# A hybrid transformer layer on one core: four weight sums moved from the retention stage into attention, one transfer for the last head's token sum, a split order and six additions on another engine

## The chip, the core and the metric

The kernel runs on one core of a Trainium2 chip. A core has engines with queues of their own that work side by side: PE (TensorE, matrix products; PEld is its weight load), DVE (VectorE), ACT (ScalarE), POOL (GpSimd) and SP (SyncE, which only issues transfers here). Each engine works through its queue in order, and an instruction whose inputs are not there holds up everything behind it. Transfers run on 16 DMA engines; those issued by SP go through one queue (q1), those issued by POOL through another (q0). The metric is the device time of one execution in microseconds (us), lower is better.

## The reference, cut to what matters

One layer over 1024 latent tokens of width 1024, with 256 context tokens:

```
h   = rms_norm(x) * (1 + sc1) + sh1                 # latent; the context likewise
p   = h @ w_in                                      # columns for two head groups
ret = silu(rg) * (group_norm(retention forwards) + group_norm(retention backwards))   # 4 heads
dif = sub_norm((softmax(q1 k1) - lam * softmax(q2 k2)) @ v)                           # 4 heads
x   = x + g1 * (concat(ret, dif) @ w_out)
h2  = rms_norm(x) * (1 + sc2) + sh2
x   = x + g2 * ((silu(a) * b) @ w_down)             # a, b: the halves of conv3(h2 @ w_up)
out = rms_norm(x) * final_g
```

All is float32. A product of the large projections is made in three passes over operands that are split into a high and a low part.

## The kernel before, in words

The work runs in stages that overlap at their edges: modulation and norms, the projections by `w_in`, retention (about 335 to 435 us of the profiled execution), differential attention (445 to 640 us), the output projection by `w_out` with the gated residual and the second norm (640 to 740 us), then the MLP.

**The output projection as seven products.** The product of tokens and `w_out` is cut into 2x2 blocks, and a Strassen-like scheme makes seven block products instead of eight. It needs sums of blocks of the weights and sums of blocks of the tokens. Both are formed in DRAM by transfers that add to what lies there (`accum_op=ALU.add`). The weights' sums are in `ws_d[0..3]` (each 128x4x512 float32): `w_terms` lists eight such additions, two halves (`k` of 0 and 2) for each of four sums; the first two sums add a block of `w_out`, and the other two are chained: `ws_d[1] += ws_d[0]`, then `ws_d[3] += ws_d[1]`. The tokens' sums are in `t1_d` to `t4_d`; `t1_d` holds minus the first half of the tokens of retention plus the second half.

**Retention.** `Pair` treats two 128-token chunks of one head; 16 pairs run as a pipeline in `outputs()` beside the query projection: `score`, `output` (PE), `squares` (ACT, and a power on POOL, L288), `gate` (four operations on DVE, L293, and two on POOL, L295 and L296), `turn` (transposed on PE, copied on ACT, stored by SP, L309). For the second half of the tokens `turn` issues one more transfer on POOL's queue, which adds the piece to `t1_d` (L311). The last step of `gate`, `last_y`, is what a weight sum is ordered behind: after the gates of pairs 1, 2, 10, 11, 12 and 13 `outputs` issues eight weight sums on POOL (L366). Each pair's keys (`rk`, L257) and values with their gates (`kvo`, L242) are loaded by SP, whose queue is in order: a load of `kvo` waits for a buffer that POOL's L296 frees, and what stands behind it in SP's queue waits along.

**Attention.** 32 units (4 heads x 8 query tiles). The first loads of a unit's queries and keys (`load(0)`, L1018 and L1021) are issued by POOL behind `last_y` of the last pair. Iteration `n` of the loop runs the 24 operations of several units by the table `TAU`; PE, DVE, ACT and SP keep exactly the order of the program there (`in_order`), while POOL's is left to the scheduler. POOL makes two small operations of each unit (L983, an input of DVE's L986, and L987, the power behind it, which ACT's L990 waits for), loads, `joined_tokens` (sums of attention's tokens, L1130 and L1132) and the first weights' low parts (L1107, L1124). `issue_after(units[n - 5].pool_ins)` puts a transfer behind L987 of unit `n - 5` in POOL's queue.

**The output projection.** `out_step` makes one block product into four PSUM tiles, `out_weights` and `sum_operand` load and split its weights and tokens: ACT makes the high part (L1106, L1336), DVE the low one (L1107, L1337). `after=(freed,)` puts the low parts of `w4` and of the sum `t4_d` behind a residual update (`freed`) in DVE's queue. Two additions complete the last head of `t4_d` (L1333, on POOL), and `gate` multiplies a finished tile by `g1` (L1345) and adds it to the rows (L1346): on DVE everywhere but in the step of `w4`, where the addition is on POOL. `norm2` scales the finished rows (L115, a power on POOL at L116, and L1231 on DVE), and `turned0` and the steps behind it transpose them on PE (L1238) for the MLP.

## Time and profile before

| | us |
|---|---|
| median of 3 runs | 1375.2 (1374.64 to 1376.37) |
| the profiled execution's own time | 1374.97 |
| its span, from the first to the last instruction | 1373.2 |
| PE busy | 1350.2 (98% of the span) |
| DVE busy | 1001.5 (73%) |
| ACT busy | 749.1 (55%) |
| POOL busy | 351.8 (26%) |

"Busy" counts a pipelined matrix product until its modelled end, so a PE that is busy all the time may still be without a pause between products or with short ones that don't show; a wait that the profile lists for PE is time in which it had nothing to do. The chain that ended last is on PE for 81% of the span. The granted clock of TensorE was 0.998 over the execution.

### The profile page before, as it was taken

To read this page: it belongs to the slowest core of one execution; us is meant where nothing else is said; L and a number is where in the kernel's file an instruction comes from. 1 tells how busy PE (TensorE), PEld (TensorE's weight loads), DVE (VectorE), ACT (ScalarE), POOL (GpSimd) and SP (SyncE) were. 2 spreads that over 40 slices of the span, in tenths; PEclk is the share of its full clock that TensorE was granted. 3 is DMA by queue.
4 is the path that set the end of the run, shared out by engine and by line. 5 is a ranking of instruction groups with operands and counts; after the bars stand their busy time and mean duration, and the time that the engine had idled before them with its cause. 6 is when DMAs were issued, how large, how long until landed. Compare 5 with 4: busy or idle time off the path is not lost.

```text
span 1373.2 us, 19870 instructions
## 1 busy us (share of the span) xinstructions
PE 1350.2 (98%) x6978; PEld 1134.5 (83%) x6978; DVE 1001.5 (73%) x1508; ACT 749.1 (55%) x1429; POOL 351.8 (26%) x440
## 2 busy tenths in 40 slices
PE   9999999999999999999999999999999999999997
PEld 6788888888888799988877888888888888888886
DVE  4746874425775898997889986777766777798857
ACT  4643312434665789987437654455554555455543
POOL 1210005403777435543131222212222210000001
PEclk9999999999999999999999999999999999999999
DMA  9567897655877877745853898988888875963523
GB/s 362 218 252 245 288 325 232 202 171 157 212 199 189 186 168 141 145 93 154 333 165 92 200 224 218 232 223 214 208 221 215 208 193 171 375 217 110 176 92 123
DMA packets 130636, 279.71 MB, mean 204 GB/s; under 512 B 13716, under 2 KB 35220, under 8 KB 129624
## 3 DMA queue, kind: packets, MB, share of 16 engines
q1 hardware_dynamic: 100440, 212.99, 45.6%
q0 software_dynamic: 29520, 64.00, 25.4%
q10 hardware_dynamic: 576, 1.44, 0.3%
q8 instruction: 55, 0.90, 0.3%
q14 instruction: 45, 0.37, 0.1%
HBM read 212.04 MB, written 69.75 MB: 205 GB/s over the span
## 4 chain that ended last, share of the span: by engine, by line
PE 81%; DVE 7%; ACT 4%; POOL 3%; issue 3%; DMA 2%; SPq 0%; POOLq 0%; DVEq 0%; ACTq 0%
PE chain L133 6%; PE chain L134 6%; PE chain L135 6%; PE c L134 5%; PE c L133 5%; PE c L135 5%; PE pv L972 4%; PE pA L940 4%; PE pn L135 3%; PE pn L134 3%; PE pn L133 3%; PE pl L133 3%; PE pl L135 3%; PE pl L134 3%; PE third L133 3%; PE third L135 3%
## 5 line engine op out<-in xcount | busy, mean ns | idle before, releaser
L1263 POOL DMA_DIRECT2D cmb<-w_up x80 | 73.6, 1142 | 175.1 <-DMA cmb<-w_up 141.7
L133 PE MATMUL pl<-hT,whi 128*128 128x512 f32 x256 | 105.4, 412 | 0.0
L133 PE MATMUL chain<-T,whi 128*128 128x512 f32 x264 | 103.1, 391 | 0.0
L134 PE MATMUL chain<-T,whi 128*128 128x512 f32 x264 | 102.8, 389 | 0.0
L135 PE MATMUL chain<-T,wlo 128*128 128x512 f32 x264 | 102.2, 389 | 0.0
L943 DVE TENSOR_REDUCE mt<-pA 128x1 f32<-128x1280 f32 x64 | 95.2, 1488 | 7.5 <-PE pA L940 6.3
L135 PE MATMUL pl<-hT,wlo 128*128 128x512 f32 x256 | 100.1, 391 | 0.0
L134 PE MATMUL pl<-hT,whi 128*128 128x512 f32 x256 | 99.9, 390 | 0.0
L947 ACT ACTIVATE p<-pA,mt 128x1280 f32<-128x1280 f32 x64 | 85.5, 1336 | 11.2 <-DVE mt L943 9.1
L940 PE MATMUL pA<-ks,qhl 128*128 128x512 f32 (+1 forms) x384 | 89.6, 368 | 1.3 <-DMA ks<-dk 0.8
L133 PE MATMUL c<-whi,ghl 128*128 128x512 f32 x232 | 90.2, 389 | 0.0
L134 PE MATMUL c<-wlo,ghl 128*128 128x512 f32 x232 | 90.2, 389 | 0.0
L135 PE MATMUL c<-whi,ghl 128*128 128x512 f32 x232 | 90.2, 389 | 0.0
L1187 ACT CAST whi<-cmb 128x512 fp32r<-128x512 f32 x60 | 37.4, 625 | 83.0 <-PE chain L134 65.1
L940 PEld LDWEIGHTS pA<-ks,qhl 128*128 128x128 f32 x384 | 67.9, 189 | 13.7 <-DVE mt L943 1.2
L972 PE MATMUL pv<-va,aT 128*128 128x128 f32 x640 | 77.4, 276 | 1.3 <-DVE yT L1001 1.0
L972 PEld LDWEIGHTS pv<-va,aT 128*128 128x128 f32 x640 | 74.0, 192 | 3.0 <-DVE yT L1001 2.1
L1187 ACT CAST whi<-wra 128x512 fp32r<-128x512 f32 x54 | 33.0, 622 | 71.7 <-PE third L134 42.3
L134 PE MATMUL third<-yT,whi 128*128 128x512 f32 x168 | 65.4, 389 | 0.0
L133 PE MATMUL third<-yT,whi 128*128 128x512 f32 x168 | 65.4, 389 | 0.0
L135 PE MATMUL third<-yT,wlo 128*128 128x512 f32 x168 | 65.4, 389 | 0.0
L133 PE MATMUL pn<-whi,hT 128*128 128x512 f32 x160 | 64.8, 405 | 0.0
(342 smaller groups left out, 3854.6 us busy)
## 6 DMA issues: line engine op xcount, KB each, us to landing
cmb<-w_up POOLq DMA_DIRECT2D x80, 256.0 KB, 6.5
wm<-w_mod SPq DMA_DIRECT2D x32, 512.0 KB, 5.7
cmb<-w_up SPq DMA_DIRECT2D x60, 256.0 KB, 5.4
raw<-w_in SPq DMA_DIRECT2D x27, 512.0 KB, 5.4
wra<-w_up SPq DMA_DIRECT2D x23, 512.0 KB, 6.2
W<-w_down SPq DMA_DIRECT2D x44, 256.0 KB, 5.5
wrb<-w_up SPq DMA_DIRECT2D x40, 256.0 KB, 3.8
ad<-s SPq DMA_DIRECT2D x20, 512.0 KB, 5.8
```

The lines of the kernel that those rows point to most:

```text
L133: mm(ps, lh, rh, start=first, stop=False, skip_group_check=more)
L134: mm(ps, lh, rl, start=False, stop=False, skip_group_check=more)
L135: return mm(ps, ll, rh, start=False, stop=last, skip_group_check=more)
L940: mm(self.pa[m][:, c0:c1], self.q[:, m, i, qs], self.k[:, m, c0:c1], start=(i == 0), stop=(i == 1))
L943: nc.vector.tensor_reduce(out=self.mt[:, m : m + 1], in_=self.pa[m][:, :LK], axis=AX.X, op=ALU.min)
L947: nc.scalar.activation(self.p[m], self.pa[m][:, :LK], AF.Exp, scale=-1.0, bias=self.mt[:, m : m + 1], accum_out=self.s[:, m : m + 1])
L972: mm(self.pv, self.aT[:, c, :], self.v[:, c, :], start=(c == 0), stop=(c == NKT - 1))
L1187: cast = nc.scalar.copy(hi, src)
L1263: nc.gpsimd.dma_start(out=o, in_=src, accum_op=ALU.add)
```

## The change

Five things are changed. (1) Two of the four weight sums, four of the eight transfers, leave the gates of pairs 10 to 13; they are issued in attention's iterations 15, 17, 21 and 28 instead. (2) The last head's two pieces of the second half are no longer added to `t1_d` one by one from `turn`; one transfer from DRAM to DRAM, `t1_d[:, 3] += yr_d[:, 3]`, does it in iteration 6, and the copy of `t1_d` to `t2_d` moves from iteration 8 to 9. (3) The first `joined_tokens` moves from iteration 11 to 12. (4) Of the four low parts of `w4`, and of the four of the sum `t4_d`, the first two are no longer put behind `freed`. (5) Six additions go from POOL to DVE: the two that complete the last head of `t4_d`, and the four residual additions in the step of `w4`.

```diff
-                if second:
+                if second and self.h < H - 1:
                     nc.gpsimd.dma_start(out=t1_d[:, self.h, o : o + 2 * P].rearrange("p (s l) -> p s l", s=2), in_=yr, accum_op=ALU.add)
...
-        w_terms = [(i, a, k) for i, a in ((0, A22), (2, A21), (1, ws_d[0]), (3, ws_d[1])) for k in (0, 2)]
+        w_terms = [(i, a, k) for i, a in ((0, A22), (2, A21)) for k in (0, 2)]
...
-                    for _ in range({1: 2, 2: 2, 10: 1, 11: 1, 12: 1, 13: 1}.get(n, 0)):
+                    for _ in range({1: 2, 2: 2}.get(n, 0)):
                         weight_sum(last_y[0])
...
-    def out_weights(srcs, sl, eng=nc.sync, low=nc.vector, lag=0, after=()):
+    def out_weights(srcs, sl, eng=nc.sync, low=nc.vector, lag=0, after=(), free=0):
...
-                for ins in after:
+                for ins in after if k - lag >= free else ():
                     order_only(part.ins, ins.ins)
...
-            if n == 8:
+            if n in (6, 9, 15, 17, 21, 28):
                 with tc.issue_after(units[n - 5].pool_ins.ins):
-                    nc.gpsimd.dma_start(out=t2_d[:, :, :], in_=t1_d[:, :, :])
+                    if n == 6:
+                        nc.gpsimd.dma_start(out=t1_d[:, H - 1, :], in_=yr_d[:, H - 1, :], accum_op=ALU.add)
+                    elif n == 9:
+                        nc.gpsimd.dma_start(out=t2_d[:, :, :], in_=t1_d[:, :, :])
+                    else:
+                        i, j, k = {15: (1, 0, 0), 17: (1, 0, 2), 21: (3, 1, 0), 28: (3, 1, 2)}[n]
+                        nc.gpsimd.dma_start(out=ws_d[i][:, k : k + 2, :], in_=ws_d[j][:, k : k + 2, :], accum_op=ALU.add)
...
-            for half, when in ((0, (11, 18, 26, 33)), (1, (16, 24, 31))):
+            for half, when in ((0, (12, 18, 26, 33)), (1, (16, 24, 31))):
...
-    def sum_operand(src, tt, half, turn=False, after=()):
+    def sum_operand(src, tt, half, turn=False, after=(), free=0):
...
-                nc.gpsimd.tensor_tensor(out=raw[:, 3, :], in0=raw[:, 3, :], in1=r32(yT[a][1][:, D // P - 1, :]), op=ALU.add)
+                nc.vector.tensor_tensor(out=raw[:, 3, :], in0=raw[:, 3, :], in1=r32(yT[a][1][:, D // P - 1, :]), op=ALU.add)
...
-            for ins in after:
+            for ins in after if k >= free else ():
                 order_only(part.ins, ins.ins)
...
-    w4 = weights(A22, freed)
-    sum_operand(t4_d, Y12, 1, after=(freed,))
+    w4 = weights(A22, freed, free=2)
+    sum_operand(t4_d, Y12, 1, after=(freed,), free=2)
...
-        gate(rows1[t], c1[t], right, ALU.subtract, nc.gpsimd)
+        gate(rows1[t], c1[t], right, ALU.subtract)
```

PE's queue holds the same instructions in the same order before and after. The scheduler places the others anew, and three places of the queues matter below.

The first is POOL's queue in the retention pairs 10 to 12 (`wsd` is `ws_d`, `qq`, `ss` and `y` are tiles of a pair). Before:

```order
L296 TENSOR_TENSOR y<-y,kvo 128x256
L366 DMA wsd_157<-wsd_156 128x1024
L288 TENSOR_TENSOR ss<-ss,mhalf 128x4
L295 TENSOR_TENSOR y<-o 128x256
L296 TENSOR_TENSOR y<-y,kvo 128x256
L366 DMA wsd_157<-wsd_156 128x1024
L266 TENSOR_TENSOR qq<-st,qd 128x512
```

and with the change:

```order
L296 TENSOR_TENSOR y<-y,kvo 128x256
L288 TENSOR_TENSOR ss<-ss,mhalf 128x4
L295 TENSOR_TENSOR y<-o 128x256
L296 TENSOR_TENSOR y<-y,kvo 128x256
L266 TENSOR_TENSOR qq<-st,qd 128x512
```

The transfers between the pairs' operations are gone; the operations themselves keep their order.

The second is POOL's queue at the end of retention, where attention's first queries (`qhl`) and keys (`ks`) are loaded; `sgd_152<-yr` is the addition to `t1_d`. Before:

```order
L296 TENSOR_TENSOR y<-y,kvo 128x256
L1018 DMA qhl<-dq_95 64x2x256
L311 DMA sgd_152<-yr 128x256
L1018 DMA qhl<-dq_95 64x2x256
L311 DMA sgd_152<-yr 128x256
L1021 DMA ks<-dk_99 64x1280 x2
L1018 DMA qhl<-dq_95 64x2x256 x2
L1021 DMA ks<-dk_99 64x1280 x2
```

and with the change:

```order
L296 TENSOR_TENSOR y<-y,kvo 128x256
L1018 DMA qhl<-dq_95 64x2x256 x2
L1021 DMA ks<-dk_99 64x1280 x2
L1018 DMA qhl<-dq_95 64x2x256 x2
L1021 DMA ks<-dk_99 64x1280 x2
```

The two additions no longer stand between the last gate and the keys.

The third is DVE's queue in the output projection, around the residual updates of the step of `w6` (the gates of `o_0` to `o_3`). Before:

```order
L1346 TENSOR_TENSOR x_2_6788<-x_2_6788,gated 128x512
L1346 TENSOR_TENSOR x_3_6789<-x_3_6789,gated 128x512
L1345 TENSOR_TENSOR gated<-o_0_6809,g_4494 128x512
L1345 TENSOR_TENSOR gated<-o_1_6810,g_4494 128x512
L1346 TENSOR_TENSOR x_0_6786<-x_0_6786,gated 128x512
L1346 TENSOR_TENSOR x_1_6787<-x_1_6787,gated 128x512
L1345 TENSOR_TENSOR gated<-o_2_6811,g_4494 128x512
L1345 TENSOR_TENSOR gated<-o_3_6812,g_4494 128x512
L1346 TENSOR_TENSOR x_2_6788<-x_2_6788,gated 128x512
L1346 TENSOR_TENSOR x_3_6789<-x_3_6789,gated 128x512
L1107 TENSOR_TENSOR wolo<-woraw,wohi 128x512 x4
L1337 SCALAR_TENSOR_TENSOR yT_4490<-raw_6794,yT_4488 128x512 x4
```

and with the change (lines 1339, 1343, 1351 and 1352 are the former 1333, 1337, 1345 and 1346):

```order
L1352 TENSOR_TENSOR x_3_6788<-x_3_6788,gated 128x512
L1107 TENSOR_TENSOR wolo<-woraw,wohi 128x512
L1339 TENSOR_TENSOR raw_6793<-raw_6793,yT_4482 128x512
L1343 SCALAR_TENSOR_TENSOR yT_4484<-raw_6793,yT_4482 128x512
L1339 TENSOR_TENSOR raw_6793<-raw_6793,yT_4484 128x512
L1107 TENSOR_TENSOR wolo<-woraw,wohi 128x512
L1343 SCALAR_TENSOR_TENSOR yT_4484<-raw_6793,yT_4482 128x512
L1351 TENSOR_TENSOR gated<-o_0_6808,g_4488 128x512
L1351 TENSOR_TENSOR gated<-o_1_6809,g_4488 128x512
L1352 TENSOR_TENSOR x_0_6785<-x_0_6785,gated 128x512
L1352 TENSOR_TENSOR x_1_6786<-x_1_6786,gated 128x512
L1351 TENSOR_TENSOR gated<-o_2_6810,g_4488 128x512
```

Two low parts of the weights and two of the tokens move ahead of these gates, with the two additions that were POOL's; the other two of each stay behind them.

More of the change, by code (lines that the diff above doesn't have):

```diff
@@ L1164 @@
                     units[v].run(o)
-                if op == "f" and n >= 9 and n not in (11, 16, 18, 24, 26, 31, 33):
+                if op == "f" and n >= 9 and n not in (12, 16, 18, 24, 26, 31, 33):
                     with tc.issue_after(units[min(n - 6, n_units - 1)].pool_ins.ins):
@@ L1319, in run, with weights @@
             pass
-    def weights(src, *after):
+    def weights(src, *after, free=0):
         sl = []
-        run(out_weights((src,), sl, after=after))
+        run(out_weights((src,), sl, after=after, free=free))
         return sl
-    def sum_operand(src, tt, half, turn=False, after=()):
+    def sum_operand(src, tt, half, turn=False, after=(), free=0):
         raw = raw0[:, 4 * half : 4 * half + 4, :]
```

## The prediction

> **What bounds the kernel now.** I read first the busy time of each engine by stretches of the execution, from the retention pairs to the MLP (the numbers in a row: its length, then the busy time and the instructions of PE, PEld, DVE, ACT, POOL, the granted clock, the DMA share, GB/s):
>
> ```profile
> 395.00:450.00 55.00, 52.19 (x285) 43.74 (x284) 30.02 (x58) 29.08 (x86) 38.88 (x44) 1.00 0.83 200
> 450.00:470.00 20.00, 18.23 (x105) 15.31 (x104) 18.48 (x22) 15.00 (x27) 9.81 (x10) 1.00 0.65 176
> 470.00:640.00 170.00, 168.89 (x1241) 155.80 (x1240) 153.00 (x203) 153.34 (x357) 78.13 (x123) 1.00 0.65 130
> 700.00:740.00 40.00, 35.07 (x173) 27.95 (x172) 32.53 (x60) 23.00 (x40) 14.22 (x15) 1.00 0.29 96
> 740.00:1360.00 620.00, 620.00 (x2742) 512.06 (x2741) 476.20 (x643) 323.71 (x488) 94.75 (x111) 1.00 0.73 200
> ```
>
> PE is the bound nearly everywhere, and its instructions do not change. So the change can only win what PE waits: 2.8 us in the first stretch, 1.8 in the second, 1.1 in attention, 4.9 in the fourth, none behind it. A saving on POOL or DVE counts where one of these waits ends on it. Second, PE's timeline names the waits (in brackets: the idle time before the row and what ended it):
>
> ```profile
> 408.44 0.68 PE L269 MATMUL pc<-xa,rk 128*128 128x128 f32 x4 [1.80 <-DMA rk<-rk]
> 449.16 1.40 PE L940 MATMUL pA<-ks,qhl 128*128 128x512 f32 x6 [0.83 <-DMA ks<-dk]
> 708.69 0.33 PE L1238 MATMUL pt<-ident,x 128*128 128x128 f32 x1 [0.21 <-DVE x L1231]
> 710.67 0.33 PE L1238 MATMUL pt<-ident,x 128*128 128x128 f32 x1 [1.66 <-DVE x L1231]
> 730.93 0.33 PE L1238 MATMUL pt<-ident,x 128*128 128x128 f32 x1 [0.83 <-DVE sm L115]
> 732.71 0.33 PE L1238 MATMUL pt<-ident,x 128*128 128x128 f32 x1 [1.45 <-DVE x L1231]
> 737.64 0.33 PE L1238 MATMUL pt<-ident,x 128*128 128x128 f32 x1 [0.79 <-DVE x L1231]
> ```
>
> Two are for transfers in retention; five, 0.21 + 1.66 + 0.83 + 1.45 + 0.79 = 4.94 us, are for the second norm, that is for DVE's queue. All seven lie where the change works.
>
> **Edit 1, the weight sums leave retention.** POOL's first sum, SP's load behind it, and the landing of the sums and of all `rk` loads:
>
> ```profile
> 398.89 0.86 POOL L366 DMA_DIRECT2D wsd<-wsd  x1
> 399.86 0.43 SPq L257 DMA_DIRECT2D rk<-rk  x1
> wsd<-wsd POOLq DMA_DIRECT2D x4, 512.0 KB, 8.4
> DMA to landing us min/median/max: 2.6/4.9/8.7
> ```
>
> The `rk` that PE waits for is issued at 399.86 and used at 408.44: about 8.5 us, where the median of ten such loads is 4.9. In that time the first 512 KB sum, which reads two operands and writes one, runs on the same DMA engines. Without it the load needs to come only 1.80 sooner, and the median is 3.6 sooner. So I take the whole **1.80 us**; the ends are 0 (the load is held by what SP issued ahead of it) and 1.80, since PE then has work. What is late next is the next pair's load, which goes out behind a POOL queue that is shorter by one sum.
>
> **Edit 2, one transfer for the last head.** POOL's queue at the end of retention:
>
> ```profile
> 435.21 0.95 POOL L311 DMA_DIRECT2D sgd<-yr  x1
> 437.23 0.88 POOL L311 DMA_DIRECT2D sgd<-yr  x1 [0.44 <-DMA yrd<-yr]
> 437.82 1.37 POOL L1021 DMA_DIRECT2D ks<-dk  x2
> ```
>
> The next rows start about 0.6 us behind each L311, and the second had a wait of 0.44 ahead of it: 0.6 + 0.44 + 0.6 = 1.6 us of the queue before the keys. PE's wait for the keys is 0.83. PE also arrives 1.80 earlier by edit 1; but POOL's four sums, about 0.6 us of its queue each, stood ahead of the same keys (2.4 us), and the keys also lose 256 KB of additions beside them. So the keys come some 4 us earlier against PE's 1.80: **0.83 us** goes, with ends of 0 (the keys move no more than PE does) and 0.83. PE's next waits, 1.77 us in the second stretch, are for DVE's and ACT's queues, which run from the same keys on, so they stay.
>
> **What edits 1 to 3 add to attention.** Five more issues on POOL (the copy to `t2_d` only moves), each behind a unit's L987:
>
> ```profile
> 534.92 2.40 PE L972 MATMUL pv<-va,aT 128*128 128x128 f32 x20
> 541.35 2.50 PE L972 MATMUL pv<-va,aT 128*128 128x128 f32 x20 [0.23 <-DVE yT L1001]
> 547.24 2.40 PE L972 MATMUL pv<-va,aT 128*128 128x128 f32 x20
> 536.29 1.66 POOL L1124 TENSOR_TENSOR yT<-woraw,yT 128x512 fp32r<-128x512 f32 x1
> 536.41 1.57 DVE L952 SCALAR_TENSOR_TENSOR r<-r,sa,nlam 128x1 f32<-128x1 f32 x1 [0.17 <-ACT p L947]
> 605.12 0.55 POOL L987 TENSOR_TENSOR ssa<-ssa,mhalf 128x1 f32<-128x1 f32 x1 [4.78 <-DVE ssa L986]
> 571.94 0.63 POOL L1021 DMA_DIRECT2D ks<-dk  x1
> 586.87 0.56 POOL L987 TENSOR_TENSOR ssa<-ssa,mhalf 128x1 f32<-128x1 f32 x1 [0.86 <-DVE ssa L986]
> ```
>
> An issue of 0.6 to 0.95 us delays the small L983 behind it, which DVE's L986 needs only in the next unit, and POOL stands idle for most of one (4.78 of some 5.8 us ahead of 605.12). That hides it. The transfers wait for earlier ones of their queue, issued 15 us or more before, while the sums land in 8.4. The cover can fail in one way: a 128x512 operation of POOL that comes while DVE starts one with two operands holds DVE up. In the fifth row a one-column operation takes 1.57 us beside POOL's, and the unit around it takes 541.35 - 534.92 = 6.4 us from one value product to the next, the one behind it 5.9. The change puts two such operations of POOL side by side in iteration 18 and parts others from their transfers. I take **0**, with ends of -0.5 (one collision fewer) and +3 (six of half a us).
>
> **Edits 4 and 5, the output projection.** DVE's timeline, with the two groups of POOL's additions and one split of ACT ahead:
>
> ```profile
> 677.62 2.99 POOL L1333 TENSOR_TENSOR raw<-raw,yT 128x512 f32<-128x512 f32 x2 [27.97 <-DMA raw<-sgd]
> 711.70 4.09 POOL L1346 TENSOR_TENSOR x<-x,gated 128x512 f32<-128x512 f32 x3
> 683.58 0.63 ACT L1336 ACTIVATE yT<-raw 128x512 fp32r<-128x512 f32 x1 [1.58 <-PE o L134]
> 678.24 1.24 DVE L1346 TENSOR_TENSOR x<-x,gated 128x512 f32<-128x512 f32 x1
> 679.40 1.77 DVE L1107 TENSOR_TENSOR wolo<-woraw,wohi 128x512 fp32r<-128x512 f32 x1
> 687.21 1.37 DVE L1345 TENSOR_TENSOR gated<-o,g 128x512 f32<-128x512 f32 x2 [3.04 <-PE o L135]
> 692.10 2.49 DVE L1107 TENSOR_TENSOR wolo<-woraw,wohi 128x512 fp32r<-128x512 f32 x4
> 694.51 2.49 DVE L1337 SCALAR_TENSOR_TENSOR yT<-raw,yT 128x512 fp32r<-128x512 f32 x4
> 710.13 0.88 DVE L1231 TENSOR_SCALAR x<-x,sm 128x512 f32<-128x512 f32 x2 [0.44 <-POOL sm L116]
> 713.34 0.69 DVE L1345 TENSOR_TENSOR gated<-o,g 128x512 f32<-128x512 f32 x1 [1.13 <-POOL x L1346]
> 713.95 2.39 DVE L1246 TENSOR_TENSOR yT<-raw,yT 128x512 fp32r<-128x512 f32 x1
> 717.75 2.44 DVE L1246 TENSOR_TENSOR yT<-raw,yT 128x512 fp32r<-128x512 f32 x2
> 737.10 0.88 DVE L1231 TENSOR_SCALAR x<-x,sm 128x512 f32<-128x512 f32 x2 [0.67 <-POOL sm L116]
> ```
>
> Four in a row take 2.49, so one is 0.60 us in DVE's queue and 0.68 alone. Six additions cost DVE 3.6 us. Beside POOL's, DVE lost (1.24 - 0.68) + (1.77 - 0.68) = 1.65 and 1.13 + (2.39 - 0.68) + (2.44 - 1.28) = 4.0, together 5.65 us, which come back. So DVE wins about 2 us.
>
> The first group of PE's waits: DVE stands idle for 3.04 us until 687.21. With the 1.65 that come back ahead of it there are 4.7 us for the two additions and four low parts that the new order puts there, 6 x 0.60 = 3.6. The last of them needs ACT's split at 683.58, which waits for PE and ends at 684.2; that leaves enough. So the gates from 692.10 on start 4 x 0.60 = 2.4 us sooner. Three low parts that stood between the scalings now follow them, 1.8 us more. I replay DVE's queue in the new order with these durations and with PE's tiles (16 groups of three products, 10.9 us a step) as inputs: the last scaling of the first rows ends near 707.5 instead of 711.0, ahead of the transposes, the first of which waits from 708.5. Both waits, **1.87 us**, go; as the margin is small, the lower end is 0.9.
>
> The second group: going on with the replay, the three low parts, four products and four additions of the step of `w4` fit before the gates of the next step, and DVE reaches the last scaling at about 733.4 instead of 737.1, 3.7 sooner. PE is 1.87 sooner itself, so the waits of 3.07 shrink by **1.85**; the ends are 0.9 (half of it) and 3.07 (all).
>
> [...]
>
> **The sum.** 1.80 + 0.83 + 0 + 1.87 + 1.85 = 6.35 us. From the profiled execution's 1374.97 (span 1373.2 and 1.77 around it; the median of the runs is 1375.2, 0.2 more) this gives **1368.6**.
>
> **The rivals.**
>
> *Attention gives half back.* The moved sums meet POOL's large operations, and six units last half a us longer: 1368.6 + 3 = 1371.6. For it: PE, DVE and ACT are within 10% of each other there (168.9, 153.0, 153.3 of 170). Against it: the new transfers stand behind the small L987, not ahead of a large operation.
>
> *The additions only change owner.* Where they ran beside single-operand work of DVE, nothing comes back for the 3.6 us that DVE takes on; the first group goes by the split order, and the second stays at 3.07: 1368.6 + 1.85 = 1370.5. For it: DVE is busy for 32.5 of 40 us there. Against it: the five stretched rows. [...]
>
> *The retention waits stay.* SP's own loads hold `rk`, and the keys follow PE: 1368.6 + 2.63 = 1371.2. For it: the longest of the ten `rk` loads took 8.7 us. Against it: the median is 4.9.
>
> *Slower: the sums delay the last head's keys.* The sum of iteration 21 goes out just ahead of the keys of the last head on POOL's queue. In retention a 512 KB sum cost `rk` about 3.6 us. The last keys, issued at 571.94, serve a unit that starts near 586 (its iteration holds the L987 at 586.87), 14 us later; the longest landing of the `rk` loads is 8.7, so it decides only once a load comes over 5 us later than that. If loads came that late and each of the four sums delayed PE by the 3.6 us, the time would be 1368.6 + 14.4 = 1383.
>
> *Nothing is won*, as DVE's queue fills again by what ACT delivers late and both transfers stay late: 1374.9 less a few tenths, 1374.
>
> **How the numbers follow.** Forecast 0.55, owner 0.11, attention 0.11, retention 0.11, nothing 0.07, slower 0.05. A difference of 0.2%, 2.75 us, is about what a measurement of this kernel can tell from no change; the forecast and the first three rivals lie beyond it, though two of them together would not. Faster 0.80, same 0.14, slower 0.06. With all upper gains (1.80 + 0.83 + 0.5 + 1.87 + 3.07 = 8.07) the time is 1366.9; the range goes from 1366.7 over the three mild rivals to 1372.6.
>
> **What would show it.** No wait of PE before `rk` near 408 and before `ks` near 447; no idle time of DVE near 684 and six rows more there; the rows of L1246 back at 0.68; the first transposes without a wait and about 1.2 us left before the second ones. In attention PE's idle time should stay near 1.1 us. The forecast is wrong if a new wait of PE for `ks` or for DVE's L952 appears in attention, or if the last scaling still ends 4 us after the last gate's tile.

## The result and the profile after

The median went from 1375.05 us (1373.73 to 1376.66, 6 runs) to **1366.55 us** (1365.44 to 1366.97, 6 runs): ratio 0.9936, 95% interval 0.9923 to 0.9949, that is 8.5 us faster (7.0 to 10.6). The profiled execution took 1366.66 us, its span is 1364.9. The forecast was 1368.6 with a range from 1366.7, so the direction was right and the size too small; the time lies just below the range.

The busy times by the same stretches as in the prediction (length, then PE, PEld, DVE, ACT, POOL, granted clock, DMA share, GB/s), changed kernel:

```profile
395.00:450.00 55.00, 55.00 (x303) 47.10 (x302) 32.59 (x63) 31.40 (x89) 35.02 (x39) 1.00 0.63 169
450.00:470.00 20.00, 18.49 (x117) 15.74 (x116) 18.87 (x23) 16.02 (x31) 10.62 (x13) 1.00 0.59 148
470.00:640.00 170.00, 169.42 (x1246) 155.98 (x1244) 150.79 (x204) 154.15 (x362) 82.09 (x126) 1.00 0.75 145
700.00:740.00 40.00, 38.87 (x200) 31.63 (x199) 36.39 (x67) 25.84 (x45) 6.88 (x9) 1.00 0.35 94
```

PE's timeline, four of the waits that are left between 440 and 740 us; the others are of 0.48 us or less (in brackets the idle time before the row and what ended it; the new lines of the kernel shift line numbers behind 1150 by 6):

```profile
458.65 0.44 PE L960 MATMUL pt<-ident,p 128*128 128x128 f32 x2 [0.68 <-DVE xa L462]
596.93 2.50 PE L972 MATMUL pv<-va,aT 128*128 128x128 f32 x20 [0.25 <-DVE yT L1001]
724.01 0.33 PE L1244 MATMUL pt<-ident,x 128*128 128x128 f32 x1 [0.36 <-DVE x L1237]
728.92 0.33 PE L1244 MATMUL pt<-ident,x 128*128 128x128 f32 x1 [0.77 <-DVE x L1237]
```

Retention has no wait left behind its first product with a formed state, the first transposes of the second norm have none, and 0.36 + 0.77 = 1.13 us are left before the second ones. DVE's timeline in the projection:

```profile
680.19 0.68 DVE L1339 TENSOR_TENSOR raw<-raw,yT 128x512 f32<-128x512 f32 x1
681.39 0.69 DVE L1343 SCALAR_TENSOR_TENSOR yT<-raw,yT 128x512 fp32r<-128x512 f32 x1
682.95 1.37 DVE L1351 TENSOR_TENSOR gated<-o,g 128x512 f32<-128x512 f32 x2 [0.88 <-PE o L135]
689.04 1.29 DVE L1343 SCALAR_TENSOR_TENSOR yT<-raw,yT 128x512 fp32r<-128x512 f32 x2
707.42 0.68 DVE L1252 TENSOR_TENSOR yT<-raw,yT 128x512 fp32r<-128x512 f32 x1
```

The moved additions and low parts fill what were 3.04 us of idle time before the gates (0.88 left), two low parts of the tokens follow the gates instead of four, and the split low part of the MLP's tokens (L1246 before, L1252 now) takes 0.68 instead of 2.4.

**Where the time went** is read best from landmarks: the starts of rows of PE that are the same in every kernel. Of the kernel before and of the changed one:

```profile
323.09 0.71 PE L269 MATMUL pc<-st,rk 128*128 128x128 f32 x4 [0.38 <-DVE st L466]
445.64 1.30 PE L940 MATMUL pA<-ks,qhl 128*128 128x512 f32 x6
465.69 2.50 PE L972 MATMUL pv<-va,aT 128*128 128x128 f32 x20 [0.24 <-ACT aT L966]
645.60 2.50 PE L972 MATMUL pv<-va,aT 128*128 128x128 f32 x20
750.51 0.60 PE L1238 MATMUL pt<-ident,x 128*128 128x128 f32 x4
```

```profile
323.16 0.71 PE L269 MATMUL pc<-st,rk 128*128 128x128 f32 x4 [0.18 <-DVE st L466]
443.20 1.30 PE L940 MATMUL pA<-ks,qhl 128*128 128x512 f32 x6
462.11 2.50 PE L972 MATMUL pv<-va,aT 128*128 128x128 f32 x20 [0.24 <-ACT aT L966]
641.32 2.50 PE L972 MATMUL pv<-va,aT 128*128 128x128 f32 x20
741.79 0.60 PE L1244 MATMUL pt<-ident,x 128*128 128x128 f32 x4
```

They are retention's first product with a formed state, attention's first scores, its first and its last product with the values, and the last transposes of the second norm. The differences are four stretches: R (retention), S (attention's start), A (attention) and P (projection with its norm). Up to 323 us both are equal, and behind the last transposes the changed kernel takes 0.4 more (622.69 and 623.11); over all kernels without and with edits 4 and 5, e3, e4, e12 and e15 left out, the means there are 622.9 and 623.0, so this is scatter. The table gives the stretches of all profiled kernels, with the parts of the change that each holds.

| kernel | edits | R | S | A | P |
|---|---|---|---|---|---|
| before | none | 122.55 | 20.05 | 179.91 | 104.91 |
| e13_swap | one transfer in attention later | 122.51 | 20.11 | 179.02 | 104.07 |
| e7_small | late sums 1/64 of the bytes | 122.48 | 20.08 | 179.90 | 103.85 |
| e6_token | 2 | 122.54 | 18.90 | 179.90 | 104.09 |
| e5_sums | 1 | 120.00 | 20.10 | 179.20 | 103.97 |
| e1_ret_att | 1, 2, 3 | 120.12 | 18.89 | 179.19 | 103.81 |
| e3_split | 4 | 122.56 | 20.54 | 180.69 | 101.95 |
| e4_adds | 5 | 123.37 | 20.11 | 179.92 | 101.77 |
| e2_proj | 4, 5 | 122.55 | 20.08 | 179.95 | 99.98 |
| changed | 1 to 5 | 120.04 | 18.91 | 179.21 | 100.47 |
| e11_after | 1 to 5 | 120.38 | 18.89 | 179.15 | 101.13 |
| e8_nosums | 1 to 5, moved sums left out | 120.09 | 18.90 | 179.88 | 100.46 |
| e9_eight | 1 to 5, eight small issues | 125.18 | 18.90 | 179.89 | 99.96 |
| e10_bytes | 1 to 5, four copies by ACT | 121.38 | 18.91 | 179.81 | 101.24 |
| e14_bytes2 | 1 to 5, two copies by ACT | 121.13 | 18.90 | 179.16 | 100.29 |
| e12_best | 1 to 5 and more | 120.08 | 18.89 | 179.13 | 100.46 |
| e15_best | 1 to 5 and more | 120.33 | 18.89 | 179.16 | 98.97 |

R, S and A repeat to some 0.1 us in most rows, which no time of a whole execution does (e4's R holds a wait of 0.78 for a gate near 355 us, e11's and e15's one of about 0.2). P scatters by about 0.6 either way. In e3 a clock of 0.91 in the stretch from 450 to 470 us lengthens S, and its A begins at a row that is listed with 3.28 us for that reason; these two are not used.

### The profile page after: what moved, and what is told of

Same layout as the page of the kernel before. It is cut to its first block, busy times and chain, and to the rows that moved or that the text cites. A ratio compares the mean times of both kernels' runs of the same rounds, so it can differ in the third digit from the quotient of the medians.

```text
span 1364.9 us, 19852 instructions
## 1 busy us (share of the span) xinstructions
PE 1348.9 (99%) x6978; PEld 1134.5 (83%) x6978; DVE 1000.7 (73%) x1514; ACT 749.6 (55%) x1429; POOL 344.2 (25%) x433
## 4 chain that ended last, share of the span: by engine, by line
PE 71%; DVE 5%; ACT 2%; issue 2%; DMA 2%; POOL 1%; POOLq 0%; DVEq 0%; ACTq 0%
PE chain L133 6%; PE chain L134 6%; PE chain L135 6%; PE c L134 5%; PE c L133 5%; PE c L135 5%; PE pv L972 4%; PE pA L940 4%; PE third L134 3%; PE third L135 3%; PE third L133 3%; PE pl L133 2%; PE pl L135 2%; PE pl L134 2%; PE pt L960 2%
```

## The experiments

**Halves and single edits of the projection.** e1 takes edits 1 to 3 into the kernel before, e2 edits 4 and 5, e3 edit 4 alone, e4 edit 5 alone, each as in the diff of the change. The microseconds given with a ratio are worked out from the ratio; the differences of the medians lie up to 0.7 us off (5.5 for e1). For e4 for example:

```diff
-                nc.gpsimd.tensor_tensor(out=raw[:, 3, :], in0=raw[:, 3, :], in1=r32(yT[a][1][:, D // P - 1, :]), op=ALU.add)
+                nc.vector.tensor_tensor(out=raw[:, 3, :], in0=raw[:, 3, :], in1=r32(yT[a][1][:, D // P - 1, :]), op=ALU.add)
...
-        gate(rows1[t], c1[t], right, ALU.subtract, nc.gpsimd)
+        gate(rows1[t], c1[t], right, ALU.subtract)
```

> Edits 1 to 3 alone (weight sums and last head's token sum out of retention, joined sum one iteration later); the projection stays as before. By the prediction's terms: 1.80 + 0.83 + 0 = 2.6 us faster. By PE's waits in the two traces (retention 2.81 to 0, attention's start 1.78 to 1.40, attention's two pv waits 0.98 to 0.49, all there while PE reaches attention's last value product 4.3 us earlier): 4.0 to 4.4 us faster. If the extra is only a difference from one profile to the next, this stays at 2.6 and the profile shows waits of some 1.77 at attention's start and 1 in attention. Rival (attention gives half back): 0 to 1 faster. The waits behind 700 us should be those of the kernel before, 4.9 us in all.

> Edits 4 and 5 alone (split order and six additions on DVE); retention and attention stay as before. By the prediction's terms 1.87 + 1.85 = 3.7 us faster, and PE's waits for rk (1.80) and ks (0.83) are there. If edits 1 to 3 and 4 to 5 add up, the sum of this run's gain and of the other half's is the 8.5 us of the whole change; if this one gives over 5, retention won nothing.

> Edit 4 alone (two of four low parts each ahead of the gates), additions stay on POOL. Theory (two separate causes): the four low parts fill DVE's idle time before the gates, the last scaling of the first rows ends ahead of the transposes, the first group of waits (1.87) goes, the second group stays near 3.07, since POOL's four additions still hold DVE's L1246 to 2.4 us: 1.9 faster. Rival (the additions are what counts, or the split low parts run into POOL's L1333 and take 2.4 us): 0 to 0.5 faster, first group still there.

> Edit 5 alone (six additions on DVE), low parts stay behind the gates. Theory (DVE wins back more than it takes on, where POOL's additions stretched its own): L1246 takes 0.68 instead of 2.4, DVE's 1.13 of idle time for POOL goes, 4.0 us back for 4 additions of 0.60, so the second group of waits (3.07) loses about 1.6; the first group (1.87) stays, as the gates still start with PE's tile and the low parts stand behind them: 1.6 faster. Rival (the additions only change owner): 0, second group still 3.07. If edits 4 and 5 need each other, e3 and e4 together give less than e2.

Against a median of 1374.01 of the kernel before (22 runs): e1 1368.55, ratio 0.9965 (0.9952 to 0.9979), 4.8 us; e2 1370.01, 0.9970 (0.9959 to 0.9982), 4.1 us; e3 1371.69, 0.9985 (0.9977 to 0.9994), 2.1 us; e4 1371.13, 0.9983 (0.9974 to 0.9992), 2.3 us. The halves add up to 8.9 us, the whole gave 8.5, and e3 and e4 add up to 4.4, about e2.

e1 gives more than the 2.6 us of the prediction's terms, and the extra is in three stretches that repeat: R falls by 2.5, S by 1.15, A by 0.7. So it is no scatter between two profiles. e3 and e4 show two causes: the split order alone takes the first group of waits away, the additions alone bring the second from 3.07 to 1.10 (0.94 + 0.16). That the additions only change owner is refuted. The second group lost 2.0 us by the additions alone, where 1.6 was expected.

**Edits 1 and 2 apart, and what edit 1 acts through.** e5 moves the four sums and nothing else, e6 takes the last head's single transfer and the later copy. e7 keeps the order of before and cuts the four late sums down; e8 takes the sums out of the changed kernel:

```diff
 # e7
-                added = nc.gpsimd.dma_start(out=ws_d[i][:, k : k + 2, :], in_=a[:, k : k + 2, :], accum_op=ALU.add)
+                if i in (1, 3):
+                    added = nc.gpsimd.dma_start(out=ws_d[i][:, k : k + 1, :16], in_=a[:, k : k + 1, :16], accum_op=ALU.add)
+                else:
+                    added = nc.gpsimd.dma_start(out=ws_d[i][:, k : k + 2, :], in_=a[:, k : k + 2, :], accum_op=ALU.add)
 # e8
-            if n in (6, 9, 15, 17, 21, 28):
+            if n in (6, 9):
```

> Edit 1 alone: the four chained weight sums go from retention to attention's iterations 15, 17, 21 and 28; the token sums stay as before. Theory: PE's wait for rk, 0.84 to 1.80 us in the four profiles so far whose retention is unchanged, goes; the wait for ks (0.53 to 0.83 there) stays or shrinks by some 0.6, as the keys come 2.4 us of POOL's queue earlier and PE 1 to 1.8 us earlier. In attention the 0.75 us wait of PE near 600 us falls to about 0.25, since with the sum of iteration 28 POOL's queue has L1107 between the two transfers of L1132 and it ends 0.7 us sooner under DVE's L1294. Together 2 to 3.5 us faster. Rival (attention's gain is due to the later joined sum, edit 3): the 0.75 stays. Rival (the wait for rk is held by SP's own queue): rk's wait stays, 0.5 us faster or less.

> Edit 2 alone: one transfer in iteration 6 in place of the last head's two, the copy to t2_d in iteration 9; the weight sums stay in retention. Theory: PE's wait for ks (0.53 to 0.83 in the four profiles with unchanged retention) goes, the one for rk (0.84 to 1.80) stays, attention keeps its 0.75 us wait near 600 us: 0.5 to 0.8 us faster, hardly to be told from no change by the times, so the profile decides. Rival (the keys are held by the weight sums, not by the last head's additions): ks's wait stays above 0.4.

> The kernel before, with the four late weight sums cut from 128x1024 to 128x16 elements each (1/64 of the bytes; most of those two sums is left out of the output). POOL issues the same instructions. If the bytes of the sums hold rk's load back, PE's wait for rk (0.84 to 1.80) goes or falls below 0.3, as in the changed kernel. If it is the place that they take in POOL's queue (0.9 us each ahead of the pair's small operations), the wait stays at 0.8 or more. The wait for ks should stay at 0.5 to 0.8 in both, as POOL's queue keeps its length.

> The changed kernel with the four chained weight sums left out altogether (those two sums are incomplete in the output). If the moved sums cost attention nothing, the stretch from attention's first value product to its last stays at 179.2 us (before: 179.9) and the span at 1365; if they hold DVE or loads up there, it gets shorter by up to 3 us. By the theory of POOL's order, without the sum of iteration 28 the 0.75 us wait near 600 us is back, so that the stretch is 179.7 to 179.9, longer than with the sums.

e5: 1370.71 against 1374.37 (17 runs), ratio 0.9977 (0.9966 to 0.9987), 3.2 us. e6: 1372.52, ratio 0.9988 (0.9978 to 0.9997), 1.6 us. In e5 the wait for `rk` is gone and R falls by 2.5, more than the wait; S stays, and ahead of the second group of `pA` at 446 us PE waits 0.99 us. A falls to 179.20, as expected of the sum of iteration 28. In e6 the wait ahead of `pA` is gone and the one for `rk` is there with 1.73; S falls by 1.15, A stays. The two add up to e1 in every stretch, so edit 3 by itself does nothing there.

e7 is the surprise. PE's two longer waits in retention, and the last line of the view of `rk` from 380 to 450 us in e7 and, for comparison, in the kernel before:

```profile
413.09 0.46 PE L277 MATMUL po<-kvo,sc 128*128 128x128 f32 x2 [0.42 <-ACT yr L307]
419.88 0.38 PE L278 MATMUL po<-S,qq 128*128 128x128 f32 x1 [0.86 <-POOL qq L266]
```

```profile
DMA to landing us min/median/max: 2.6/2.8/5.0
```

```profile
DMA to landing us min/median/max: 3.5/8.4/8.5
```

The loads of `rk` land in 2.8 us in the median instead of 8.4, and PE's wait for them is gone, just as in the changed kernel. But R is 122.48, as long as before: PE waits 0.42 and 0.86 for other things a little later. So the bytes of the sums made the wait that the profile named, and yet were not what the stretch was worth. What is left of the sums in e7 is their issue on POOL's queue and transfers of 8 KB. POOL's timeline in e5 (no sums), and in e7:

```profile
400.73 0.74 POOL L295 TENSOR_TENSOR y<-o 128x256 f32<-128x256 f32 x1 [1.32 <-DMA kvo<-kvg]
401.55 0.73 POOL L296 TENSOR_TENSOR y<-y,kvo 128x256 f32<-128x256 f32 x1
402.23 1.30 POOL L266 TENSOR_TENSOR qq<-st,qd 128x512 f32<-128x512 f32 x1
403.49 1.02 POOL L288 TENSOR_TENSOR ss<-ss,mhalf 128x4 f32<-128x4 f32 x1
405.83 0.73 POOL L295 TENSOR_TENSOR y<-o 128x256 f32<-128x256 f32 x1 [1.32 <-DVE o L293]
```

```profile
401.80 0.72 POOL L295 TENSOR_TENSOR y<-o 128x256 f32<-128x256 f32 x1 [1.32 <-PE pl L135]
402.61 0.73 POOL L296 TENSOR_TENSOR y<-y,kvo 128x256 f32<-128x256 f32 x1
403.28 0.88 POOL L367 DMA_DIRECT2D wsd<-wsd  x1
403.93 1.55 POOL L266 TENSOR_TENSOR qq<-st,qd 128x512 f32<-128x512 f32 x1
405.19 1.29 POOL L288 TENSOR_TENSOR ss<-ss,mhalf 128x4 f32<-128x4 f32 x1
407.79 0.73 POOL L295 TENSOR_TENSOR y<-o 128x256 f32<-128x256 f32 x1 [1.32 <-DVE o L293]
```

POOL has no pause there but the 1.32 us in which DVE makes the gates from the power (L288) that POOL has just delivered. From one L295 to the next it is 5.10 us without an issue and 5.99 with one. The same four rounds of POOL, from the L295 near 395 us on (L296 in e9), in five kernels:

| kernel | issues | 1st | 2nd | 3rd | 4th | sum | R |
|---|---|---|---|---|---|---|---|
| before | four, 512 KB | 6.76 | 5.99 | 7.44 | 7.56 | 27.75 | 122.55 |
| e7_small | four, 8 KB | 6.76 | 5.99 | 7.45 | 7.51 | 27.71 | 122.48 |
| e5_sums | none | 5.89 | 5.10 | 7.42 | 6.63 | 25.04 | 120.00 |
| changed | none | 5.90 | 5.11 | 7.45 | 6.64 | 25.10 | 120.04 |
| e9_eight (below) | eight, 8 KB | 7.61 | 6.85 | 7.62 | 8.34 | 30.42 | 125.18 |

The rounds are as long with small sums as with large ones, and R follows their sum. An issue makes a round 0.85 to 0.92 us longer, but not the third (two issues there cost 0.17 in e9), where POOL waits for ACT ahead of L288 anyway (1.52 us in the changed kernel, 1.05 in before). So POOL's queue sets the pace of these pairs wherever it has no such pause, whatever PE is seen to wait for.

e8 shows that the moved sums cost attention nothing, and more: without them A is 179.88 again, and the wait of 0.76 near 597 us is back, as expected.

**Issues or bytes.** Two tests of that reading, beside the changed kernel again as a control. e9 puts two tiny transfers behind each of the gates of pairs 10 to 13, e10 puts the bytes on another queue:

```diff
 # e9
+                    if n in (10, 11, 12, 13):
+                        for e in (0, 16):
+                            added = nc.gpsimd.dma_start(out=ws_d[1][:, n - 10 : n - 9, e : e + 16], in_=ws_d[0][:, n - 10 : n - 9, e : e + 16], accum_op=ALU.add)
+                            order_only(added.ins, last_y[0].ins)
 # e10
+                    if n in (10, 11, 12, 13):
+                        moved = nc.scalar.dma_start(out=spare_d[n - 10][:, 0:3, :], in_=ws_d[0][:, 0:3, :])
+                        order_only(moved.ins, last_y[0].ins)
```

> The changed kernel with eight more transfers of 128x16 elements on POOL's queue, two behind each of the gates of pairs 10 to 13 (where the kernel before has one 128x1024 sum each); they add into 128x16 pieces of a weight sum, so those columns of the output are off. Theory that has come up from e7 (POOL's queue is a closed loop there: the power L288, 1.32 us of DVE's gates, L295, L296, the issue, L266, the next L288; each issue lengthens it by its 0.6 us): from retention's first product pc<-st,rk near 323 us to attention's first product pA the stretch is 120.0 without issues, 122.5 with four, so 124.5 to 125.0 with eight, and PE waits for POOL's qq, while rk lands in 2.6 to 4 us. Rival (the bytes of the sums hold rk up, and what e7 showed is a wait that a single issue brings): 122.5 or less.

> The changed kernel with four copies in DRAM of 128x1536 elements each (768 KB read, 768 KB written, the bytes of a 512 KB sum with its two operands) issued from ACT's queue at pairs 10 to 13; POOL issues nothing more. Theory (POOL's issues set the pace, the bytes only fill a wait that is there anyway): rk lands late again (over 6 us), but the stretch from pc<-st,rk near 323 us to pA stays within 0.7 of 120.0, plus what ACT's four issues cost. Rival (bytes alone cost as much as the issues; the two limits lie side by side): PE waits for rk by 1 us or more and the stretch is 121.0 to 122.5.

e9 has R = 125.18, that is 5.14 us above the changed kernel for eight issues, **0.64 us each** in the mean; the four of e7 cost 122.48 - 120.04 = 2.44, 0.61 each. `rk` is no issue in it (it lands in 4.2 at most), and PE waits for DVE, ACT and POOL's `qq` instead. In e10 the rival holds: R is 121.38, and PE waits 1.06 for `rk`. SP's issue of that load and PE's row:

```profile
399.12 0.42 SPq L258 DMA_DIRECT2D rk<-rk  x1
406.55 0.68 PE L270 MATMUL pc<-xa,rk 128*128 128x128 f32 x4 [1.06 <-DMA rk<-rk]
```

Both are the fifteenth of the sixteen pairs. The trace has no landing for this load, but PE's wait for it ended about 7.3 us behind its issue; in the changed kernel the same load, issued at 399.97, landed in 3.8. So the load is late beside bytes of another queue too. ACT's queue had another order of its own in e10, and so it was repeated with the bytes ahead of the place (e14, below).

**Attention's 0.7 us.** e13 is the kernel before with the second transfer of one joined sum issued behind POOL's next low part (L1107), which is where the changed kernel has it:

```diff
+            if (h, half) == (2, 0) and to is t3_d:
+                late.append((to[:, h, :], raw))
+            else:
                 nc.gpsimd.dma_start(out=to[:, h, :], in_=raw, accum_op=ALU.add)
...
                         next(wo_gen, None)
+                        if late:
+                            low = [i for i in nc.cur_bb.bb.instructions[-8:] if i.engine == nc.gpsimd.engine][-1]
+                            o, raw = late.pop()
+                            order_only(nc.gpsimd.dma_start(out=o, in_=raw, accum_op=ALU.add).ins, low)
 # e14, in the changed kernel's retention
+                    if n == 9:
+                        for i in (0, 2):
+                            moved = nc.scalar.dma_start(out=spare_d[i][:, :, :], in_=ws_d[i][:, :, :])
+                            order_only(moved.ins, last_y[0].ins)
```

> The kernel before with one edit: of the two transfers of the joined sum in iteration 26, the second goes out behind POOL's L1107 (as it stands in the changed kernel, where the sum of iteration 28 follows); nothing else moves. Theory (L1107, a 128x512 operation of POOL, holds DVE's small L1294 until it ends; one issue earlier it ends earlier): L1294 takes 1.45 instead of 2.12 us or less, PE's wait of 0.75 near 601 us falls to 0.25, the stretch from attention's first value product to its last is 179.2 as in the changed kernel, instead of 179.9. Rival (attention's gain has to do with the moved sums or the shorter queue behind them): 179.9 and 0.75.

> The changed kernel with two plain copies in DRAM of 1 MB each (1 MB read, 1 MB written each) issued together from ACT's queue just ahead of the place of the first late weight sum; POOL issues nothing more. They should run for some 15 to 20 us beside the loads of pairs 11 to 14. Theory (POOL's issues set the pace; the bytes by themselves cost little): stretch from pc<-st,rk near 323 us to pA 120.0 to 120.8. Rival (the bytes hold the loads up): rk lands in over 6 us, PE waits for it, 121.5 or more.

POOL's and DVE's timelines in the kernel before, in the changed one and in e13:

```profile
595.75 1.96 POOL L1107 TENSOR_TENSOR wolo<-woraw,wohi 128x512 fp32r<-128x512 f32 x1
595.62 2.12 DVE L1294 TENSOR_SCALAR m<-m 128x8 f32<-128x8 f32 x1
```

```profile
591.81 1.59 POOL L1107 TENSOR_TENSOR wolo<-woraw,wohi 128x512 fp32r<-128x512 f32 x1
592.00 1.45 DVE L1300 TENSOR_SCALAR m<-m 128x8 f32<-128x8 f32 x1
```

```profile
593.93 1.60 POOL L1107 TENSOR_TENSOR wolo<-woraw,wohi 128x512 fp32r<-128x512 f32 x1
594.36 1.21 DVE L1303 TENSOR_SCALAR m<-m 128x8 f32<-128x8 f32 x1
```

DVE's operation on eight columns ends 0.03 to 0.05 us behind POOL's each time (597.74 and 597.71, 593.45 and 593.40, 595.57 and 595.53). What ties the two ends is not shown; in before DVE's row starts 0.13 us ahead of POOL's. One issue of POOL less ahead of L1107 lets both end sooner: counted from the start of the L983 ahead of it in POOL's queue (594.19, 590.81 and 592.94), L1107 ends after 3.52 us in before and after 2.59 in the two others. A is 179.02 in e13, and PE's waits near 600 us are gone. So all of attention's gain is the place of one POOL operation, which the sum of iteration 28 moved by the way. Such a gain is easily lost: in e9 L1304, which is L1300 of the changed kernel, takes 1.45 as there, but a later operation of DVE on one column takes 1.86 and ends with a large one of POOL (627.90 and 627.89), PE waits 0.73 at 631.28, and A is 179.89. In e10 A is 179.81 without such a row; why was not followed up.

e7 to e10, e13 and e14 were each timed once: 1373.76, 1366.55, 1371.03, 1368.56, 1372.15 and 1367.08 us. What they show is in their traces.

e14: R = 121.13, between the two expectations; 0.48 of it is a wait of PE for a low part of weights. The load of `rk` beside the copies lands in 7.8, and PE does not wait for it. So the copies by ACT lengthen retention by about 1.1 and 1.3 in two forms, issues alone by 2.44, and both together (before) by 2.51: they are two limits side by side, and the two do not add. How much of the 1.1 to 1.3 is bytes and how much is the changed order of ACT's queue stays open.

**A version that beats both.** PE's last two waits, 1.13, come from the end of the projection. PE finished the last row's tile at about 721.2, but its gate stood in DVE's queue until 724.87. e12 makes two low parts of the MLP's tokens behind that gate and moves L1300 a unit earlier; e15 drops the latter, and also sets the order of the two halves of the last scalings and makes one shifted tile on ACT:

```diff
 # e12 and e15
-            split_to(raw0[:, d, :], (B11, B21)[d // 4], d % 4)
+            if d < KD - 2:
+                split_to(raw0[:, d, :], (B11, B21)[d // 4], d % 4)
...
-        gate(rows1[t], c1[t], left, ALU.subtract)
+        freed = gate(rows1[t], c1[t], left, ALU.subtract)
...
+    for d in (KD - 2, KD - 1):
+        split_to(raw0[:, d, :], B21, d % 4)
+        order_only(nc.cur_bb.bb.instructions[-1], freed.ins)
 # e15
-            turned(0, d, raw0[:, d, :], d % 2 == 0)
+            turned(0, d, raw0[:, d, :], d % 2 == 0 or d == KD - 1)
...
+            if c and t >= NT - 2:
+                order_only(last_scaled[0].ins, prev[0].ins)
```

> The changed kernel again, as the control for e12 on the same chip: 1366.5 us, 0.9930 to 0.9945 of the kernel before.

> The changed kernel with two more moves: in the last step of the projection the gate of the last row goes ahead of two low parts (L1252) of the MLP's tokens in DVE's queue, and the factor of the second norm (L1300) is computed one unit of attention earlier, where POOL has no large operation. Theory: the last row's gate starts 1.2 us sooner, the row before it 0.6, so the two waits of PE for the second norm's rows (0.36 + 0.77 = 1.13) shrink to 0.4 or less; the wait of 0.25 near 597 us goes. 0.9 to 1.3 us below e11. Rival (the chain from ACT's square over POOL's power to the scaling sets these waits, not DVE's order): within 0.3 of e11.

> The changed kernel with DVE's order at the end of the projection as in e12, and with what e12 had wrong: both halves of the last two rows are scaled in the order in which PE needs them, with no other operation between, the last row's gate goes out as soon as PE's tile is there, and the last of the eight shifted tiles is made by ACT instead of DVE. The factor of the second norm is back at its place. Theory (DVE's order sets PE's last waits): the stretch from PE's last o product to its last pt takes 20.0 to 20.3 instead of 20.8 us (e12: 21.3), PE waits 0.5 or less there instead of 1.13 (e12: 1.64); 0.5 to 0.8 faster than the changed kernel, 0.9930 to 0.9937 of the kernel before, not to be told from the changed one by the times. Rival (the chain of square, power and scaling sets it): 20.8 or more.

e11: 1366.07 against 1373.29 (9 runs), ratio 0.9941 (0.9928 to 0.9955). e12: 1366.22, 0.9947 (0.9934 to 0.9959), no gain. DVE and PE in e12:

```profile
725.62 0.49 DVE L1237 TENSOR_SCALAR x<-x,sm 128x512 f32<-128x512 f32 x1 [0.66 <-POOL sm L116]
726.02 0.68 DVE L1197 TENSOR_TENSOR wlo<-wrb,whi 128x512 fp32r<-128x512 f32 x1
726.63 0.48 DVE L1237 TENSOR_SCALAR x<-x,sm 128x512 f32<-128x512 f32 x1
```

```profile
727.16 0.33 PE L1244 MATMUL pt<-ident,x 128*128 128x128 f32 x1 [1.46 <-DVE x L1237]
```

Counted from PE's last `o` product, the last row was scaled 1.2 us sooner than in the changed kernel, but the half that PE needs first came second, behind a low part, and PE's transposes had been placed earlier as well: PE waits 1.46 instead of 0.77. L1300 a unit earlier took the wait of 0.25 away, but A stayed at 179.13: no gain.

e15: **1364.36** against 1374.14 (9 runs), ratio 0.9926 (0.9913 to 0.9940). PE has no wait left before the second norm's rows, and from PE's last `o` product to its last `pt` it takes 19.58 us instead of 20.82. Some 0.6 of that are given back behind it (623.76 us to the end instead of 623.11). It is the fastest kernel here, though by its interval not to be told from the changed one.

## Why the prediction was right, and too small

**The projection** (1.87 + 1.85 = 3.72) was right in both mechanisms and, as a sum, in the size. The split order fills DVE's idle time and takes the first group; the additions on DVE free the low parts and take 1.94 of the second group's 3.07, leaving 1.13 where 1.2 were forecast. By P over the kernels without edits 4 and 5 (six rows, mean 104.12) and with both (seven rows, mean 100.50; e12 and e15 left out) the gain is 3.6. The profile of before was a high one here: its first group was 1.87, the five others with the same code had 1.04 to 1.23, while in these five the second group cost more than its waits (see the last section). From the last `o` product to the last `pt` the gain is 2.2 us against the profile of before and 2.5 to 2.7 against these five, where the second term was 1.85. So that the sum came out this near is in part luck: for these five its first term was too large and its second too small.

**Edit 1** failed at the step "I take the whole 1.80 us; the ends are 0 ... and 1.80, since PE then has work". R fell by 2.5. The listed wait for `rk` was made by the bytes of the sums, as the prediction said, but it stood in front of another limit, POOL's queue with four issues of 0.61 to 0.64 us in the mean; e7 takes the wait away and keeps the time, e9 doubles the issues and doubles the cost. Bytes without issues on POOL cost about 1.1 to 1.3 at most (e10, e14). The prediction had the right term at hand ("POOL's four sums, about 0.6 us of its queue each", 2.4 us) and used it only for the keys. (Its median of 4.9 is that of the seven of the ten loads for which the trace has a landing.) A listed wait bounds what its own removal can bring, not what the removal of another limit can, and short waits don't show at all: in before, PE's listed waits in R are 1.98 us, and the stretch is 2.5 longer.

**Edit 2** was right in the wait for `ks`, but "PE's next waits, 1.77 us in the second stretch, ... stay" was not: S fell by 1.15 instead of 0.83. The wait for DVE's `xa` went from 1.06 to 0.68, so part of it came from the same late keys.

**Attention** was taken at 0 "with ends of -0.5 (one collision fewer) and +3". One collision became shorter (2.12 to 1.45 us), and that was worth 0.7, more than the end of -0.5. That a small operation of DVE can be held beside a large one of POOL was in the prediction, from one row of L952 (1.57 us for one column, where the median of the 32 is 0.22); that the order of POOL's queue around iteration 26 decides another such pair was to be seen only by following each of the large operations, which was not done. PE's idle time there is 170 - 169.42 = 0.6 us instead of the 1.1 that was to stay. No new wait of PE appeared and the last head's keys were not late, so neither the rival in attention nor the slower one came about.

**The sum.** 2.5 + 1.15 + 0.7 + 3.6 = 7.95 by the stretches, against 6.35 forecast; the median of 8.5 lies half a us further, inside its interval of 7.0 to 10.6. The low end of the range, 1366.7, was set by the sum of all upper gains taken from listed waits; it left out both the limits behind the waits and the scatter of a median of about 1 us.

## What to carry to other kernels

A wait that the profile names is what came last, not what the stretch costs: before pricing its removal, look for a second engine that has no pause of its own there, and count what the change takes off that queue, each issue included. To see which limit is the longer one, take the first away and leave the second, as e7 does. Compare stretches between landmarks of the busiest engine over several profiles; they repeat to 0.1 us where times of whole executions scatter by 2 to 3, and so let single edits of half a us be told apart. Where two engines collided here, POOL's L1107 and DVE's L1294, the order of one queue by a single issue decided when both ended (0.9 us of A between before and e13); an edit upstream may move such a place.

## What the runs showed of the hardware

- Issuing a transfer that adds in DRAM made a round of POOL's queue 0.85 to 0.92 us longer where POOL had no pause, with 8 KB as with 512 KB: four of 8 KB cost retention as much as four of 512 KB (2.44 and 2.51 us, 0.61 to 0.64 an issue in the mean, since one of the four falls into a pause).
- Loads of `rk` landed later beside large transfers in DRAM, whichever queue issued them. The load that PE waits for in before took 8.4 us to land beside 512 KB sums issued by POOL and about 7.3 beside 768 KB copies issued by ACT (e10), against 3.8 in the changed kernel; the load ahead of it took 7.8 beside 1 MB copies (e14).
- Two waits of PE in a row cost more than themselves in e1: they were 0.82 and 1.45 us, and behind them the granted clock fell, to 0.66 from 725 to 730 us. The busy times around the place, and PE's rows:

```profile
720.00:725.00 5.00, 3.18 (x14) 2.17 (x13) 4.55 (x11) 4.19 (x8) 1.50 (x2) 0.99 0.27 105
725.00:730.00 5.00, 4.55 (x16) 3.71 (x17) 3.60 (x8) 2.29 (x5) 0.55 (x1) 0.66 0.24 86
```

```profile
726.58 0.63 PE L135 MATMUL chain<-yT,wlo 128*128 128x512 f32 x1
727.00 0.63 PE L133 MATMUL second<-yT,whi 128*128 128x512 f32 x1
...
728.56 0.39 PE L134 MATMUL second<-yT,whi 128*128 128x512 f32 x1
728.78 0.39 PE L135 MATMUL second<-yT,wlo 128*128 128x512 f32 x1
```

Products start 0.42 us apart instead of 0.22 for some 3 us, about 1.2 us lost, and the third wait of before (0.79) is not there, since PE comes later. In e5, e6, e7 and e13 a stretch of 5 us at or behind the same two waits has a clock of 0.66 to 0.82 as well; in the profile of before, behind waits of 0.83 and 1.45, it stayed at 1.00. The length of the waits does not decide it, and what does is not shown. The second group cost about the same either way: 22.99 us from the last `o` product to the last `pt` in before, 23.3 to 23.5 in those.
